# Value products of a whole pair of heads at a time, spatial mixing placed earlier, and first-norm vectors by float32r products

## The chip, the cores and the metric

The kernel runs on one core of one Trainium2 chip. The metric is device microseconds of one execution, launch to end; the profiled execution also has a span, the time from its first to its last instruction. TensorE (PE) does the matrix products and the transpositions, with its weight loads as a row of their own (PEld); VectorE (DVE), ScalarE (ACT) and GpSimd (POOL) do the element work; SyncE (SP) and ACT issue the transfers. Each engine runs its instructions in the order in which the program has them, and waits at an instruction whose inputs are not there.

## The reference, cut to what matters

```python
D_MODEL, SEQ, DEPTH = 1024, 512, 2          # x is (1, 512, 1024) float32

def gqa_attention(q, k, v):                 # 8 query heads of 64, 2 key/value heads, no mask
    sc = einsum('bqkgd,bskd->bkgqs', qi, k) * scale
    p = softmax(sc, axis=-1)
    return einsum('bkgqs,bskd->bqkgd', p, v)

def spatial_gating(u, v, ln_g, ln_b, w_s, b_s):   # 4 chunks of 128 rows, 8 groups of 64 columns
    vn = layer_norm(v, ln_g, ln_b)
    mixed = einsum('gmn,bcngd->bcmgd', w_s, vc) + b_s
    return u * mixed

def hybrid_layer(x, ...):
    hcat = x @ w_in + b_in
    na_q, na_k, na_v, na_z, gq_q, gq_k, gq_v, gq_z, sg_u, sg_v, sg_z, gates = split(hcat)
    p_a = (neighbourhood_attention(na_q, na_k, na_v) * silu(na_z)) @ w_br_a
    p_b = (gqa_attention(rope(rms_norm(gq_q)), rope(rms_norm(gq_k)), gq_v) * silu(gq_z)) @ w_br_b
    p_c = (spatial_gating(sg_u, sg_v) * silu(sg_z)) @ w_br_c
    g = sigmoid(gates)
    merged = g[0] * p_a + g[1] * p_b + g[2] * p_c
    return layer_norm(alpha * x + merged @ w_out + b_out, ln_g, ln_b)

h = layer_norm(x, ln_in_g, ln_in_b)         # the first norm
for l in range(DEPTH):
    h = hybrid_layer(h, ...)
```

## The kernel before, in words

All activations stay on the chip. A projection of float32 accuracy is three float32r products, high by high, low by high and high by low (L196, L197, L198), where the high part is a rounded copy made on ACT (`whi_*`, L143; `xh`, L249) and the low part the rest, made on DVE (`wlo_*`, L144; `xl`, L250). Weights come in chunks of 128 x 1024 (512 KB), eight (or four) of them to a projection, each in turn loaded by SP, split on ACT and DVE and multiplied.

**Order of the work.** `main` hands steps to a scheduler (`step(...)`), which fixes the order of the instructions of each engine when the program is built. The loop of one layer (from L928) first hands over ten chunks, the values of the spatial gating `sg_value`, those of the neighbourhood attention `na_value` and the first two gates of branch B (`zb_0`, `zb_1`), with the norms, rotations and stacking of the GQA queries and keys between them (list `between`, L934). Then come 16 units of GQA, one to a pair of heads `hp` (0 to 3) and a chunk of 128 queries `t` (0 to 3), with projections and the spatial mixing put between their steps (list `fill`, L944).

**One GQA unit** has, for the two heads e = 0, 1 of the pair: scores `gs` (L703 and L704, 512 keys), the row maximum `nm` on DVE (L706), Exp to `gp` with its row sum on ACT (L709), the division on DVE (`ri` L715, `gp` L716), four transpositions into one PSUM tile `gt` (L723) and its copy `gpT` to SBUF on ACT (L725, a ring of six buffers). After every second unit (`n % 2 == 0`, L962) the value products of the two units before it are handed over: `gqa_value`, tile `gy` (L735), which for each block of 128 keys has one product for e = 0 that writes the upper 64 partitions and one for e = 1 that writes the lower 64. A float32 product leaves two records in the trace, so one unit has 16 records of `gy`, which start two by two.

**Spatial gating**, `sg_mix(l, c)` for the four chunks c: `norm` transposes the projected values into PSUM (`svT`, L524) and takes their statistics on DVE (`st_sg`, L223 to L226); `mix` normalises by two DVE instructions (`vn`, L233 and L235), multiplies by the spatial weights (`mix`, L536, eight products of 64 columns, in the same two halves as `gy`) and adds the bias on DVE (L540, four instructions).

**Neighbourhood attention** comes later, between the projections of gates and branches: scores `ns`, transpositions `nT` with their copies to `npT` (two buffers of 128 x 896, L792 to L798), and value products `ny` (L810, L817), again in two halves.

**The start**, `first_layer_start` (L319): gain and bias of the first norm come as one row (`lnrow`, 8 KB, L323); four float32 products with a row of ones (`lnb`, L347) spread them over 128 partitions in PSUM; DVE applies them to the first rows of x (L359 and L361, twice each); then the transpositions `xt_in` (L365) and the first query products `gq` (L306). The raw weights are split by `high` (ACT, L337) and `low` (POOL for q0 and q1, DVE for q2 and q3, L340). The statistics of a norm end on POOL with a power (`rs_*`, L226).

## Time and profile before

| | |
|---|---|
| median of 3 runs | 1092.2 us (1090.23 to 1094.16) |
| the profiled execution, its own time | 1090.98 us |
| its span | 1089.2 us |
| busy share of PE, PEld, DVE, ACT, POOL | 99%, 82%, 59%, 43%, 5% |
| chain of work that ended last | PE 97%, DVE 2% |
| mean granted clock of TensorE | 0.998 of 2.4 GHz |

The span is the measure for the sum of a change, because starts and lengths are given in it. Matrix products overlap in the pipeline, so that the length of one in the trace (0.39 us for 512 columns) is longer than its distance to the next one's start (0.23 us); distances between starts are what a product costs. A busy PE in these rows is one with a product in the pipeline, which leaves room for bubbles between starts that no wait shows.

### The profile page before, as it was taken

The numbers are of one execution on the slowest core, as the hardware profiler recorded it, in microseconds if no ns is written. First come the engines' busy times: TensorE is split into PE (matmuls) and PEld (weight loads), VectorE is DVE, ScalarE is ACT, GpSimd is POOL, SyncE is SP. The second block draws the span as 40 slices with busy tenths as digits, with TensorE's granted clock in tenths as the row PEclk, the third lists the DMA queues.
The fourth block names the chain that finished last, engine by engine and source line by source line (L and its number), as shares of the span: only waits on it lengthen the run. The fifth ranks groups of instructions, "written<-read, shape, count | busy, mean of one in ns | idle before, by whom it ended". The sixth has DMA issues, their size and how long they took to land.

```text
span 1089.2 us, 14738 instructions
## 1 busy us (share of the span) xinstructions
PE 1075.7 (99%) x5744; PEld 887.8 (82%) x5744; DVE 640.5 (59%) x1205; ACT 470.6 (43%) x841; POOL 52.8 (5%) x54
## 2 busy tenths in 40 slices
PE   8999999999999999999999999999999999999997
PEld 5988788888888888888888887888888888888886
DVE  6775956665554543546876478566555555344465
ACT  4245735555655422334422365455645643223320
POOL 4420000000000000000021000000000000000001
PEclk9999999999999999999999999999999999999999
DMA  7522322213333433335652332222233334333421
GB/s 284 165 78 82 100 97 59 59 55 91 115 111 117 137 97 97 108 105 174 231 180 58 97 110 73 78 58 58 86 102 87 115 117 135 97 97 97 135 78 58
DMA packets 142808, 116.59 MB, mean 107 GB/s; under 512 B 4881, under 2 KB 130321, under 8 KB 142737
## 3 DMA queue, kind: packets, MB, share of 16 engines
q1 hardware_dynamic: 141872, 113.21, 33.5%
q10 hardware_dynamic: 866, 2.43, 0.6%
q8 instruction: 45, 0.74, 0.3%
q14 instruction: 25, 0.20, 0.1%
HBM read 109.34 MB, written 6.29 MB: 106 GB/s over the span
## 4 chain that ended last, share of the span: by engine, by line
PE 97%; DVE 2%; DMA 0%; issue 0%; ACT 0%; DVEq 0%
PE gq L306 4%; PE gy L735 3%; PE gb L196 3%; PE gc L198 3%; PE gc L197 3%; PE po L198 3%; PE po L197 3%; PE po L196 3%; PE gc L196 3%; PE ga L198 3%; PE ga L196 3%; PE gb L198 3%; PE gb L197 3%; PE ga L197 3%; PE gt L723 3%; PE gs L703 2%
## 5 line engine op out<-in xcount | busy, mean ns | idle before, releaser
L706 DVE TENSOR_REDUCE nm<-gs 128x1 f32<-128x512 f32 x64 | 42.3, 684 | 26.9 <-PE gs L704 26.8
L709 ACT ACTIVATE gp<-gs,nm 128x512 f32<-128x512 f32 x64 | 43.8, 688 | 21.4 <-DVE nm L706 19.8
L198 PE MATMUL gc<-xh,wlo_gc 128*128 128x512 f32 x128 | 51.1, 399 | 0.0
L725 ACT ACTIVATE gpT<-gt 128x512 f32<-128x512 f32 x64 | 36.7, 598 | 31.0 <-PE gt L723 30.8
L197 PE MATMUL gc<-xl,whi_gc 128*128 128x512 f32 x128 | 50.0, 391 | 0.0
L196 PE MATMUL gc<-xh,whi_gc 128*128 128x512 f32 x128 | 50.0, 391 | 0.0
L196 PE MATMUL gb<-xh,whi_gb 128*128 128x512 f32 x128 | 50.0, 391 | 0.0
L198 PE MATMUL gb<-xh,wlo_gb 128*128 128x512 f32 x128 | 49.8, 389 | 0.0
L197 PE MATMUL gb<-xl,whi_gb 128*128 128x512 f32 x128 | 49.8, 389 | 0.0
L196 PE MATMUL ga<-xh,whi_ga 128*128 128x512 f32 x128 | 49.8, 389 | 0.0
L198 PE MATMUL ga<-xh,wlo_ga 128*128 128x512 f32 x128 | 49.8, 389 | 0.0
L197 PE MATMUL ga<-xl,whi_ga 128*128 128x512 f32 x128 | 49.8, 389 | 0.0
L226 POOL TENSOR_TENSOR rs_po<-rs_po,pw 128x1 f32<-128x1 f32 x8 | 7.5, 939 | 814.4 <-DVE rs_po L225 814.4
L143 ACT ACTIVATE whi_gb<-raw_gb 128x1024 fp32r<-128x1024 f32 x16 | 17.0, 1060 | 60.4 <-PE pb L197 22.7
L779 ACT ACTIVATE nt<-nt,mx 128x256 f32<-128x256 f32 x64 | 30.1, 471 | 23.3 <-DVE mx L775 22.7
L144 DVE TENSOR_TENSOR wlo_ga<-raw_ga,whi_ga 128x1024 fp32r<-128x1024 f32 x16 | 19.6, 1222 | 33.5 <-ACT whi_ga L143 33.5
L735 PE MATMUL gy<-gpT,gv 128*64 128x128 f32 x512 | 38.8, 279 | 0.0
L723 PE MATMUL gt<-ident,gp 128*128 128x128 f32 x256 | 37.4, 276 | 0.7 <-ACT gpT L725 0.7
L735 PEld LDWEIGHTS gy<-gpT,gv 128*64 128x64 f32 x512 | 29.6, 136 | 10.2 <-issue 8.3
L144 DVE TENSOR_TENSOR wlo_gb<-raw_gb,whi_gb 128x1024 fp32r<-128x1024 f32 x16 | 19.6, 1222 | 30.1 <-ACT whi_gb L143 29.9
L723 PEld LDWEIGHTS gt<-ident,gp 128*128 128x128 f32 x256 | 29.7, 140 | 8.6 <-issue 2.7
L306 PE MATMUL gq<-w_gq,xh 128*128 128x512 f32 x128 | 34.0, 398 | 0.0
(282 smaller groups left out, 3099.0 us busy)
## 6 DMA issues: line engine op xcount, KB each, us to landing
raw_o<-in_w_out SPq DMA_DIRECT2D x24, 512.0 KB
raw_gc<-in_w_in SPq DMA_DIRECT2D x16, 512.0 KB
raw_gb<-in_w_in SPq DMA_DIRECT2D x16, 512.0 KB
raw_ga<-in_w_in SPq DMA_DIRECT2D x16, 512.0 KB
raw_gq<-in_w_in SPq DMA_DIRECT2D x8, 512.0 KB
raw_sv<-in_w_in SPq DMA_DIRECT2D x8, 512.0 KB
raw_nv<-in_w_in SPq DMA_DIRECT2D x8, 512.0 KB
raw_zb<-in_w_in SPq DMA_DIRECT2D x8, 512.0 KB
```

The costliest lines, as they stand in the source:

```text
L144: dve.tensor_tensor(wlo, raw, asf(whi), op=ALU.subtract)
L196: pe.matmul(ps, lhsT=lhi, rhs=rhi, start=first, stop=False)
L197: pe.matmul(ps, lhsT=lhi, rhs=rlo, start=False, stop=False)
L198: pe.matmul(ps, lhsT=llo, rhs=rhi, start=False, stop=last)
L306: pe.matmul(ps, lhsT=x[:, k, tk], rhs=w[p][k], start=n + k == 0, stop=n == 2 and k == KD - 1)
L703: pe.matmul(ps, lhsT=lhs, rhs=st["ks"][:, g, 0, :], start=True, stop=False)
L706: dve.tensor_reduce(out=nm, in_=ps, axis=AX.X, op=ALU.max, negate=True)
L709: act(pt, ps, AF.Exp, bias=nm, accum_out=sm)
L723: pe.transpose(ps[:, P * k:P * k + P], pt[:, P * k:P * k + P], ident)
L725: act(pT, ps, AF.Copy)
L735: pe.matmul(ps[64 * e:64 * e + 64, P * t:P * t + P], lhsT=st["gv"][:, k, HD * g:HD * g + HD], rhs=st["gp", hp, t, e][:, P * k:P * k + P], ...
L779: act(T[:, cs], T[:, cs], AF.Exp, bias=mx[:, i:i + 1], scale=SCALE, accum_out=sm[:, i:i + 1])
```

## The change

It has four parts. (1) The start: gain and bias are loaded spread over 128 partitions (`lnflat`, 256 KB instead of 8 KB), rounded on ACT, their rest taken on POOL, and `lnb` becomes eight float32r products over 32 partitions each, with ones of 1/32. (2) The low part of weight chunk q3 goes from DVE to POOL, ahead of the second statistics. (3) `gqa_value` is handed over once per pair of heads, four units together, the ring `gpT` has nine buffers, and `npT` takes two buffers of that ring instead of its own. (4) The norms and mixes of the spatial gating are handed over one by one between projections, the first before `zb_0` and before `zb_1`, and the third gate of B, `zb_2`, comes earlier.

```diff
@@ -86,8 +86,8 @@
     pw = cst.tile([P, 10], F32, name="pw")
     pool.memset(pw, -0.5)
 
-    one = cst.tile([P, 1], F32, name="one")
-    pool.memset(one, 1.0)
+
+
     bcol = cst.tile([P, DEPTH, NCOL], F32, name="bcol")
     hcol = cst.tile([P, DEPTH, NCOL], F32, name="hcol")
     bvg = cst.tile([P, DEPTH, NKV], F32, name="bvg")
@@ -319,8 +319,12 @@
     def first_layer_start():
         raw = {}
         input_load(0)
-        rows = rp.tile([P, 2, D], F32, tag="r8", name="lnrow")[0:1]
-        scalar.dma_start(rows, a["ln_in_rows"])
+        rows = rp.tile([P, 3, S], F32R, tag="r8", name="lnrow")
+        one = rows[:, 2, 0:P]
+        pool.memset(asf(one), 1.0 / 32)
+        R = a["ln_in_rows"]
+        flat = t2("lnflat")
+        scalar.dma_start(flat, bass.AP(tensor=R.tensor, offset=R.offset, ap=[[S, 4], [0, 32], [1, S]]))
         scalar.dma_start(ident, a["ident"])
         for n in ("q0", "q1", 1, "q2", "q3", 2, "k0", 3, "k1"):
             if isinstance(n, int):
@@ -341,11 +345,16 @@
 
         gains = {}
         lnc = st["lnc"] = cst.tile([P, 2, D], F32, tag="cvec", name="lnc_in")
-        for h in range(2):
-            for j in range(2):
-                ps = gains[j, h] = psum("acc" if h + j < 2 else "att", f"lnb_{h}_{j}")
-                pe.matmul(ps, lhsT=one[0:1].broadcast_to([1, P]), rhs=rows[:, j, 512 * h:512 * h + 512],
-                          start=True, stop=True)
+        act(rows[:, 0], flat, AF.Copy)
+        pool.tensor_tensor(rows[:, 1], flat, asf(rows[:, 0]), op=ALU.subtract)
+        for p in range(2):
+            for h in range(2):
+                for j in range(2):
+                    q = 64 * h + 32 * j
+                    if p == 0:
+                        gains[j, h] = psum("acc" if h + j < 2 else "att", f"lnb_{h}_{j}")
+                    pe.matmul(gains[j, h], lhsT=one[q:q + 32], rhs=rows[q:q + 32, p],
+                              start=p == 0, stop=p == 1)
 
         def stats(i):
             st["stats", i] = row_stats(st["xin", i], D, f"in{i}")
@@ -377,9 +386,9 @@
         apply(0)
         high("q2")
         low("q2", dve)
+        high("q3")
+        low("q3", pool)
         stats(1)
-        high("q3")
-        low("q3", dve)
         for kc in range(4):
             st["gqw", kc] = w[f"q{kc}"]
         gq_queries(0, 0)
@@ -721,7 +730,7 @@
         ps = psum("att", f"gt_{l}_{hp}_{t}_{e}")
         for k in range(NT):
             pe.transpose(ps[:, P * k:P * k + P], pt[:, P * k:P * k + P], ident)
-        pT = tp.tile([P, S], F32, tag="gpT", name=f"gpT_{l}_{hp}_{t}_{e}", bufs=6)
+        pT = tp.tile([P, S], F32, tag="gpT", name=f"gpT_{l}_{hp}_{t}_{e}", bufs=9)
         act(pT, ps, AF.Copy)
         st["gp", hp, t, e] = pT
 
@@ -789,13 +798,14 @@
 
     def na_transpose(l, hp, e):
         T = st["np", hp, e]
-        pT = tp.tile([P, 896], F32, tag="pT", name=f"npT_{l}_{hp}_{e}", bufs=2)
+        pT = []
         for j, n in ((0, 4), (1, 3)):
             ps = psum("att", f"nT_{l}_{hp}_{e}_{j}")
             for k in range(n):
                 c = P * (4 * j + k)
                 pe.transpose(ps[:, P * k:P * k + P], T[:, c:c + P], ident)
-            act(pT[:, 512 * j:512 * j + P * n], ps[:, 0:P * n], AF.Copy)
+            pT.append(tp.tile([P, S], F32, tag="gpT", name=f"npT_{l}_{hp}_{e}_{j}", bufs=9))
+            act(pT[j][:, 0:P * n], ps[:, 0:P * n], AF.Copy)
         st["np", hp, e] = pT
 
     def na_out(l, hp):
@@ -809,13 +819,13 @@
                     h = 2 * hp + e
                     pe.matmul(ps[64 * e:64 * e + 64, P * i + 64:P * i + 192],
                               lhsT=v[:, i + kb, HD * h:HD * h + HD],
-                              rhs=st["np", hp, e][:, 256 * i + P * kb:256 * i + P * kb + P],
+                              rhs=st["np", hp, e][i // 2][:, 256 * (i % 2) + P * kb:256 * (i % 2) + P * kb + P],
                               start=kb == 0, stop=kb == 1)
         for q0, kt, c in ((448, 3, 768), (0, 0, 832)):
             for e in range(2):
                 h = 2 * hp + e
                 pe.matmul(ps[64 * e:64 * e + 64, q0:q0 + 64], lhsT=v[:, kt, HD * h:HD * h + HD],
-                          rhs=st["np", hp, e][:, c:c + 64], start=True, stop=True)
+                          rhs=st["np", hp, e][1][:, c - 512:c - 448], start=True, stop=True)
         u = t2(f"nyo_{l}_{hp}")
         dve.scalar_tensor_tensor(out=u, in0=ps, scalar=bias(l, C_NAV + P * hp), in1=st["zs", "a", hp],
                                  op0=ALU.add, op1=ALU.mult)
@@ -930,19 +940,20 @@
         step(lambda l=l: layer_constants(l))
         chunks = [sg_value(l, f) for f in range(4)] + [na_value(l, f) for f in range(4)]
         chunks += [z_gate(l, "b", C_GZ, j) for j in range(2)]
-        M, R, T = gq_moments, gq_rotate, gq_stack
-        between = [[(M, 0)], [(M, 1)], [(R, 0)], [(T, 0), (M, 2)], [(R, 1)], [(T, 1), (M, 3)], [(R, 2)],
-                   [(T, 2), (R, 3)], [(T, 3)], []]
+        norm, mix = [list(fs) for fs in zip(*[sg_mix(l, c) for c in range(NCHUNK)])]
+        M, R, T = [[lambda i=i, f=f, l=l: behind_start(l, f, i) for i in range(NT)]
+                   for f in (gq_moments, gq_rotate, gq_stack)]
+        between = [[M[0]], [M[1]], [R[0]], [T[0], M[2]], [R[1]], [T[1], M[3]], [R[2]], [T[2], R[3]],
+                   [T[3], norm[0]], [mix[0], norm[1]]]
         for c, fs in zip(chunks, between):
-            for f, i in fs:
-                step(lambda l=l, f=f, i=i: behind_start(l, f, i))
+            for f in fs:
+                step(f)
             step(*c)
-        (n0, m0), (n1, m1), (n2, m2), (n3, m3) = [[(f,) for f in sg_mix(l, c)] for c in range(NCHUNK)]
         z = {j: z_gate(l, "b", C_GZ, j) for j in (2, 3)}
         u = [sg_out_u(l, j) for j in range(4)]
         g = [sg_out_z(l, j) for j in range(4)]
-        fill = [n0, na_q(l, 0), n1, m0, n2, na_k(l, 0), m1, n3, m2, m3, u[0], u[1], g[0], u[2], z[2], g[1],
-                u[3], z[3], g[2], g[3]]
+        fill = [na_q(l, 0), (mix[1],), (norm[2],), na_k(l, 0), (mix[2],), (norm[3],), z[2], (mix[3],), u[0], u[1], g[0],
+                u[2], g[1], u[3], z[3], g[2], g[3]]
         units = [(hp, t) for hp in range(NPAIR) for t in range(NT)]
         at = done = 0
         total = sum(len(f) - 1 for f in fill)
@@ -959,8 +970,8 @@
                 step(*fill[at])
                 done += len(fill[at]) - 1
                 at += 1
-            if n > 0 and n % 2 == 0:
-                for u in units[n - 2:n]:
+            if n > 0 and n % NT == 0:
+                for u in units[n - NT:n]:
                     step(lambda l=l, u=u: gqa_value(l, *u))
 
         rest = []
@@ -1046,7 +1057,7 @@
     arrays = {n: np.ascontiguousarray(v[n]) for n in _DIRECT}
     arrays["x"] = np.ascontiguousarray(v["x"].reshape(ROWS, 8, 8, D).transpose(1, 0, 2, 3).reshape(S, D))
     arrays["b_cols"] = np.ascontiguousarray(v["b_in"].reshape(DEPTH, NCOL, P).transpose(2, 0, 1))
-    arrays["ln_in_rows"] = np.ascontiguousarray(np.stack([v["ln_in_g"], v["ln_in_b"]])[None])
+    arrays["ln_in_rows"] = np.ascontiguousarray(np.stack([v["ln_in_g"], v["ln_in_b"]]).reshape(2, 2, S).transpose(1, 0, 2))
     bv = v["b_in"][:, C_GV:C_GV + P].reshape(DEPTH, NKV, HD).transpose(2, 0, 1)
     arrays["b_gv"] = np.ascontiguousarray(np.concatenate([bv, bv], axis=0))
     arrays["rpb"] = np.ascontiguousarray(np.pad(v["na_rpb"][:, :, ::-1, :], ((0, 0), (0, 0), (0, 0), (RPB_PAD, RPB_PAD))))
```

Lines move by up to 11: `gs` is L712 and L713 after the change, `nm` L715, `gt` L732, `gy` L744, `mix` L545, `svT` L533, `lnb` L356; L143 to L310 stay.

**PE, the place of the first mixing product of layer 0.** `mix_0` is the mixing of chunk 0 and reads `vn_0`; `zb_0` and `zb_1` are gates of branch B, `nq_0` a projection of the neighbourhood queries, `gs_e_t` scores. Before, from the first gate's last product on:

```order
...
L524 MATMUL svT_0_997<-ident,sv_520 128x128 x4
L703 MATMUL gs_0_0_974<-ks_502,qs_0_500 128x512
L198 MATMUL zb_1_944<-xh,wlo_zb_1_903 128x512
...
L704 MATMUL gs_1_0_982<-ks_502,qs_0_500 128x512
L196 MATMUL nq_0_1016<-xh,whi_nq_0_938 128x512
...
L198 MATMUL nq_0_1016<-xh,wlo_nq_0_939 128x512
L524 MATMUL svT_1_1049<-ident,sv_520 128x128 x4
L536 MATMUL mix_0_1064<-sgc_493,vn_0_1061 64x128 x8
```

Now:

```order
L498 MATMUL kT_636<-ident,qk_3_750 128x128
L533 MATMUL svT_0_909<-ident,sv_526 128x128 x4
L196 MATMUL zb_0_927<-xh,whi_zb_0_851 128x512
...
L713 MATMUL gs_0_1_1167<-ks_508,qs_0_506 128x512
L712 MATMUL gs_1_1_1175<-ks_508,qs_0_506 128x512
L713 MATMUL gs_1_1_1175<-ks_508,qs_0_506 128x512
L545 MATMUL mix_0_960<-sgc_499,vn_0_957 64x128 x8
L533 MATMUL svT_1_973<-ident,sv_526 128x128 x4
L196 MATMUL zb_1_991<-xh,whi_zb_1_921 128x512
```

`svT_0` moved ahead of the 24 products of `zb_0`, and `mix_0` ahead of the 24 of `zb_1` and the 24 of `nq_0`: between `kT` and `mix_0` there are now `svT_0`, `zb_0` and eight products of scores. Layer 1 has the same order.

**DVE, the instructions that end in `vn_0`.** `ks` and `qs` are the low parts of stacked keys and queries, `nm_e_t` row maxima of scores, `wlo_nq_0` the low part of a weight chunk. Before:

```order
L505 TENSOR_TENSOR ks_502<-kT_630,ks_502 64x512
L496 TENSOR_TENSOR qs_1_501<-qT_3_880,qs_1_501 64x2x128
L223 BN_STATS st_sg_0_1002<-svT_0_997 128x6
L144 TENSOR_TENSOR wlo_nq_0_939<-raw_nq_0_797,whi_nq_0_938 128x1024
...
L233 SCALAR_TENSOR_TENSOR vn_0_1061<-svT_0_997,mv_sg_0_1003,sgc_493 128x512
L706 TENSOR_REDUCE nm_0_0_977<-gs_0_0_974 128x1
L706 TENSOR_REDUCE nm_1_0_985<-gs_1_0_982 128x1
L235 SCALAR_TENSOR_TENSOR vn_0_1061<-vn_0_1061,rs_sg_0_1004,sgc_493 128x512
```

Now:

```order
L514 TENSOR_TENSOR ks_508<-kT_636,ks_508 64x512
L505 TENSOR_TENSOR qs_1_507<-qT_3_886,qs_1_507 64x2x128
L233 SCALAR_TENSOR_TENSOR vn_0_957<-svT_0_909,mv_sg_0_915,sgc_499 128x512
L715 TENSOR_REDUCE nm_0_0_1024<-gs_0_0_1021 128x1
L144 TENSOR_TENSOR wlo_nq_0_986<-raw_nq_0_803,whi_nq_0_985 128x1024
L715 TENSOR_REDUCE nm_1_0_1032<-gs_1_0_1029 128x1
L715 TENSOR_REDUCE nm_0_1_1170<-gs_0_1_1167 128x1
L715 TENSOR_REDUCE nm_1_1_1178<-gs_1_1_1175 128x1
L235 SCALAR_TENSOR_TENSOR vn_0_957<-vn_0_957,rs_sg_0_916,sgc_499 128x512
```

The statistics of `svT_0` moved ahead of the last `ks`, and two more row maxima stand ahead of the second instruction of `vn_0`, the last of them that of the scores right ahead of `mix_0` on PE.

**POOL at the start.** `rs_in` is the power that ends the statistics of a row block. Before:

```order
L226 TENSOR_TENSOR rs_in_136<-rs_in_136,pw 128x1
L340 TENSOR_TENSOR w_gq_0_142<-raw_gq_0_107,w_gq_0_142 128x1024
L340 TENSOR_TENSOR w_gq_1_145<-raw_gq_1_109,w_gq_1_145 128x1024
L226 TENSOR_TENSOR rs_in_171<-rs_in_171,pw 128x1
```

Now:

```order
L349 TENSOR_TENSOR lnrow<-lnflat,lnrow 128x512
L226 TENSOR_TENSOR rs_in_142<-rs_in_142,pw 128x1
L344 TENSOR_TENSOR w_gq_0_148<-raw_gq_0_107,w_gq_0_148 128x1024
L344 TENSOR_TENSOR w_gq_1_151<-raw_gq_1_109,w_gq_1_151 128x1024
L344 TENSOR_TENSOR w_gq_3_175<-raw_gq_3_115,w_gq_3_175 128x1024
L226 TENSOR_TENSOR rs_in_180<-rs_in_180,pw 128x1
```

The rest of gain and bias stands ahead of the first power, and the low part of q3 ahead of the second.

## Rows read from the trace of the kernel before

**Rows 1.** The page: busy time, share of the span and instructions of each engine.

```profile
PE 1075.7 (99%) x5744; PEld 887.8 (82%) x5744; DVE 640.5 (59%) x1205; ACT 470.6 (43%) x841; POOL 52.8 (5%) x54
```

**Rows 2.** The waits of PE: line, releaser, us in total, times, longest.

```profile
PE lnb L347 <- DMA lnrow<-in_ln_in_rows: 3.5, 1, 3.5
PE xt_in L365 <- DVE xin L361: 1.8, 2, 0.9
PE gt L723 <- ACT gpT L725: 0.7, 2, 0.4
PE nk L196 <- DVE vn L233: 0.2, 1, 0.2
```

**Rows 3.** Timeline of PE at a value group: start, us, what.

```profile
182.97 0.39 PE L198 MATMUL sz<-xh,wlo_sz 128*128 128x512 f32 x1
183.29 1.97 PE L735 MATMUL gy<-gpT,gv 128*64 128x128 f32 x32
...
185.53 0.40 PE L704 MATMUL gs<-ks,qs 128*128 128x512 f32 x1
185.76 0.39 PE L703 MATMUL gs<-ks,qs 128*128 128x512 f32 x1
```

**Rows 4.** The same group, asked for a stretch inside it (183.7 to 184.6).

```profile
183.45 1.37 PE L735 MATMUL gy<-gpT,gv 128*64 128x128 f32 x22
```

**Rows 5.** Timeline of PE at a value group that holds one pair of records.

```profile
134.56 0.40 PE L704 MATMUL gs<-ks,qs 128*128 128x512 f32 x1
134.89 0.43 PE L735 MATMUL gy<-gpT,gv 128*64 128x128 f32 x2
135.25 0.50 PE L703 MATMUL gs<-ks,qs 128*128 128x512 f32 x1
135.59 0.40 PE L704 MATMUL gs<-ks,qs 128*128 128x512 f32 x1
```

**Rows 6.** Timeline of PE: the last key transposition and the first mixing of layer 0.

```profile
97.41 0.27 PE L489 MATMUL kT<-ident,qk 128*128 128x128 f32 x1
...
116.47 1.09 PE L536 MATMUL mix<-sgc,vn 128*64 128x128 f32 x16
```

**Rows 7.** Timeline of DVE from behind the last stacked keys to vn, layer 0.

```profile
104.89 0.42 DVE L496 TENSOR_TENSOR qs<-qT,qs 64x256 fp32r<-64x256 f32 x1
...
105.96 1.21 DVE L144 TENSOR_TENSOR wlo_nq<-raw_nq,whi_nq 128x1024 fp32r<-128x1024 f32 x1
...
109.57 1.29 DVE L706 TENSOR_REDUCE nm<-gs 128x1 f32<-128x512 f32 x2 [0.31 <-PE gs L704]
110.77 0.74 DVE L235 SCALAR_TENSOR_TENSOR vn<-vn,rs_sg,sgc 128x512 f32<-128x512 f32 x1
```

**Rows 8.** Timeline of the start, PE, DVE and POOL.

```profile
3.53 7.16 PE L347 MATMUL lnb<-lnrow,one 1*128 1x512 f32 x8 [3.53 <-DMA lnrow<-in_ln_in_rows]
...
7.30 4.66 POOL L340 TENSOR_TENSOR w_gq<-raw_gq,w_gq 128x1024 fp32r<-128x1024 f32 x2 [0.18 <-ACT w_gq L337]
...
9.02 0.75 DVE L359 SCALAR_TENSOR_TENSOR xin<-xin,mv_in,lnb 128x512 f32<-128x512 f32 x1 [0.90 <-PE lnb L347]
...
10.72 0.75 DVE L361 SCALAR_TENSOR_TENSOR xin<-xin,rs_in,lnb 128x512 f32<-128x512 f32 x1 [0.96 <-PE lnb L347]
...
12.42 1.80 PE L306 MATMUL gq<-w_gq,xh 128*128 128x512 f32 x4
...
14.06 1.09 PE L306 MATMUL gq<-w_gq,xl 128*128 128x512 f32 x4
```

**Rows 9.** Stretches: us, busy PE, PEld, DVE, ACT, POOL, granted clock, DMA share, GB/s.

```profile
10.00:12.00 2.00, 2.00 (x7) 1.19 (x7) 0.75 (x1) 0.23 (x1) 1.96 (x1) 1.00 1.03 406
...
1082.00:1084.00 2.00, 0.01 (x1) 0.00 (x0) 1.85 (x6) 0.00 (x0) 0.43 (x1) 1.00 0.00 0
1084.00:1086.00 2.00, 0.00 (x0) 0.00 (x0) 2.00 (x4) 0.00 (x0) 0.49 (x1) 0.89 0.00 0
```

**Rows 10.** Timeline of DVE: the four additions behind a mixing.

```profile
119.15 0.87 DVE L540 TENSOR_TENSOR m<-mix,sgc 128x128 f32<-128x128 f32 x4
```

## The prediction

> **What bounds the kernel now.** I read the page first. PE is busy for 1075.7 us, 99% of the span [rows 1], so nothing is gained by making another engine faster; time can only come from PE's own stream. The waits of PE come to 6.2 us in the whole execution: 3.5 for the first transfer, 1.8 for the first norm, 0.9 for a copy `gpT` and a `vn` [rows 2]. The third view is the timeline of PE, read by distances between starts. A product of 512 columns starts 0.23 us behind the one before it (185.76 less 185.53 [rows 3]). Inside a group of value products two records, one of each half, make a pair. The group of 32 ends at 183.29 + 1.97 = 185.26 [rows 3], the 22 records from 183.45 on end at 184.82 [rows 4], so the last 8, four pairs, take 0.44: 0.11 us a pair. What costs more is going in and out. From the product ahead of the group of 16 pairs to the second product behind it pass 185.53 - 182.97 = 2.56 us [rows 3], where paces alone give 0.23 + 16 x 0.11 + 0.23 = 2.22: 0.34, and 0.36 with one more digit, is the price of **one excursion** into half-width products and back. A group of a single pair makes it plain: 135.59 - 134.56 = 1.03 against 0.23 + 0.11 + 0.23 = 0.57 [rows 5], 0.46 for an excursion that also splits a unit.
>
> **Parts 3 and 4, excursions.** Walking the whole trace in this way, a layer has 22 excursions for `gy` and `mix`, nine at 0.36 and thirteen that split a unit at 0.40 to 0.46, together 8.6 us; and five for `ny`, 1.1 us. In the changed order I count eight for `gy` and `mix`: three mixes alone, three whole pairs of heads, and the first pair of heads in two pieces (one with the last mix in it). Six at 0.36 and two at 0.42 are 3.0 us. `ny` has one more than before, 0.45. Saved: 8.6 - 3.0 - 0.45 = 5.2 us a layer, **-10.4 us**. The number of products is the same, and the ring of nine buffers only has to hold the eight copies of a pair of heads and one more; the four units' copies, 0.6 us each on an ACT that is 43% busy [rows 1], are spread over the products of a whole pair. Bounds: -9 (each excursion at 0.31) to -12 (0.42).
>
> **Old waits.** The two `gt` waits and the `nk` wait [rows 2] stand where the second and third mix of before crowd the units. With mixes spread they go: **-0.9 us**; bounds 0 and -1.6.
>
> **Part 4, a new wait.** This is the step on which the result turns. `mix_0` was started at 116.47 [rows 6], while the `vn` that it reads was done at 110.77 + 0.74 = 111.5 [rows 7]: 5 us of slack, made by the 24 products of `zb_1` and the 24 of `nq_0` that stood ahead. In the new order these come behind it. Behind the last key transposition, at 97.41 [rows 6], PE has four transpositions of `svT` (0.5 us), 24 products of `zb_0` and eight of scores: 32 x 0.23 = 7.3. With the way into the half-width products and out of the transpositions it is ready for `mix_0` at about 105.5. DVE is not. Its clock there is set by the stacked keys, whose last instruction ends as `qs` starts, 104.89 [rows 7]; the small statistics instructions moved ahead of it add 0.1. Then come, in the new order, `qs` 0.42, the first `vn` 0.74, one row maximum 0.65, `wlo_nq` 1.21, three row maxima at 0.65, the second `vn` 0.74: 5.7 us, to about 110.7 [rows 7]. All their inputs from PE and ACT are there before their turn, save the last maximum's, whose scores end just ahead of `mix_0`. PE waits 110.7 - 105.5 = **5.2 us**, in each layer, since the order is the same in both: **+10.4 us**. Queued behind `mix_0` on PE are `svT_1`, `zb_1`, `nq_0` and everything after them, so nothing else fills the hole. Later `mix` instructions have between 5 and 11 us of products between their `svT` and themselves, and DVE ahead of them is shorter, so they wait for nothing. Bounds for both layers: +3.0 (below, first rival) to +13.
>
> **A second, small wait.** `zb_2` now follows `mix_2` with some ten products and eight transpositions between, and takes over a PSUM buffer that DVE's additions (0.87 for four [rows 10]) must leave; with a `wlo` of 1.21 [rows 7] and another instruction between them they end 2 to 3 us behind `mix_2`, PE comes after some 2.5. I take 0.4 a layer, **+0.8 us**; bounds 0 and +3.
>
> **Parts 1 and 2, the start.** `lnb` runs from 3.53 to 10.69; two of the four instructions of DVE's first apply wait 0.90 and 0.96 for it, and the last ends at 11.47 [rows 8]. In the new form: the transfer is 31 times as large, 248 KB more, 0.6 us at the 406 GB/s of this stretch [rows 9]; a rounded copy on ACT, a subtraction on POOL (2.33 for 128 x 1024 in [rows 8], so about 1.2 for half of it), and eight products, together ready at about 7. Of the two waits, 1.86, I take 1.3 as gone, since the power that ends the statistics now stands behind the subtraction on POOL and holds the second instruction a little. Further on PE waits 1.8 us for the second apply [rows 2]. DVE reaches that apply 1.2 earlier, without q3's low part (1.21 for such an instruction [rows 7]); but the power on POOL that it needs now stands behind that same low part, 2.33 there, which cannot begin before ACT has rounded q3. So I let the second apply move by the same 1.3 and not more. The start gives **-1.3 us**; bounds +0.7 (the larger transfer late, POOL in the way) and -2.8.
>
> **The clock.** The last product of the program ends at 1082.01; the granted clock is 1.00 over 1082 to 1084 with PE idle, and 0.89 over 1084 to 1086 [rows 9], so it fell from 2.4 to 1.2 GHz towards the end of that second stretch. A wait of 5.2 us at `mix_0` would reach past that. What low clock costs is in the start: four products start over 14.06 - 12.42 = 1.64 us, 0.41 each, where the pace later is 0.23 [rows 8, 3], a loss of 0.72 for the four; the transpositions ahead of them are slow too. I take twice that for one fall, and one fall for the two waits: **+1.5 us**; bounds 0 and +7 (two falls, each for 14 products and more).
>
> **The sum.** -10.4 - 0.9 + 10.4 + 0.8 - 1.3 + 1.5 = +0.1 on the profiled execution's 1090.98: 1091.1, rounded to **1091.0 us**. That execution stands 1.2 us (0.1%) below the median of the three runs shown, inside their spread. About 0.3% (3.3 us) is what a measurement of this kernel can tell from no change.
>
> **Rivals.** (1) *The wait at `mix_0` is short.* The least that it can be: the last row maximum needs the last scores, so 0.65 + 0.74 [rows 7] and the hand-over follow PE's own work, 1.5 us a layer, if DVE is otherwise done. Then the clock stays too: 1091.1 - 2 x (5.2 - 1.5) - 1.5 = **1082 us**. For it: DVE is only 59% busy, and small shifts of ACT and DVE ahead of the keys would come through at once; against it: seven of the eight instructions behind the keys take 0.65 or more, and DVE runs them with no gap over 0.31 [rows 7]. (2) *The clock falls in both waits*, at `mix_0` of both layers, decided by whether the clock goes down within the wait as it did in the idle end of the run. It costs 3.0 us a layer if the low stretch is twice as long as I took it, 1091.1 - 1.5 + 6.0 = **1096 us**, slower than before. For it: the end of the run [rows 9] where the clock held for less than 5.2 us; against it: one fall at the end says little on how sharp the point is, and the half-width products and transpositions that follow the wait are cheap to slow. The Trainium skill, page "TensorE: Matmul & The Clock Gate", section "What's actually happening", has the array's clock gated to half once it has been idle and released by sustained work; by that rule both waits fall and this rival is the forecast. The end of this trace agrees with the fall, and no row here shows one in the middle of a run. (3) *Excursions are saved and the start fails*: +0.7 in place of -1.3, **1093 us**, no change.
>
> **How the numbers follow.** Forecast with rival 3, a balance of the saved excursions and the new wait: 0.50. Rival 1 or something between it and the forecast, below 1087.7 (1091.0 less 3.3): 0.27. Rival 2, above 1094.3: 0.23. The range reaches from rival 1 to rival 2 with its bounds on the excursions, 1082 to 1097.5. Faster 0.27, within 0.3% 0.50, slower 0.23.
>
> **What would show it.** The waits of PE should have a new row, `mix` for DVE's `vn` at L235, two times, near 5 us each, and those of `gt` and `nk` should be gone; `xt_in` should wait about as long as before, with the first `gq` 1.3 us earlier; a granted clock below 1.00 in a stretch just behind one of the waits; groups of 32 `gy` records, 28 excursions in place of 54. The forecast is wrong if the `mix` wait is under 3 us, if excursions inside long groups cost more than 0.36, or if another wait above 2 us stands behind a `gt`, `nT` or `zb`.

## The result, and the profile after

| | before | after |
|---|---|---|
| median of the timed runs | 1091.45 us (5 runs) | 1100.68 us (5 runs, 1099.9 to 1100.99) |
| the profiled execution, its own time | 1090.98 us | 1099.9 us |
| its span | 1089.2 us | 1097.7 us |
| PE waits, sum of the rows | 6.2 us | 25.5 us |

The changed kernel is slower: the ratio is 1.0082 (95% interval 1.0068 to 1.0095), 9 us. The forecast was 1091.0 us and a range to 1097.5; the time is above both.

The waits of PE after the change, to be read against [rows 2]: line, releaser, us in total, times, longest.

```profile
PE lnb L356 <- ACT lnrow L348: 11.5, 1, 11.5
PE mix L545 <- DVE vn L235: 9.2, 2, 4.6
PE xt_in L374 <- DVE xin L370: 3.3, 4, 1.7
PE gt L732 <- ACT gpT L734: 1.0, 2, 0.6
PE lnb L356 <- POOL lnrow L349: 0.5, 1, 0.5
```

Two rows are new and large. The wait of `mix` for `vn` is the one that was forecast, twice 4.6 us. The first row was not: `lnb` waits 8 us longer than before for its vectors. PE is busy for 10.9 us less than before [rows 1], 5.6 of them in `lnb` itself (7.16 before, two times 0.80 now), and for all that the span is longer:

```profile
PE 1064.8 (97%) x5744; PEld 889.1 (81%) x5744; DVE 642.1 (58%) x1204; ACT 470.1 (43%) x842; POOL 56.1 (5%) x56
```

What was saved, and more, went into waiting. The timeline of the start after the change (start, us, engine, what; the bracket is the idle time before and what ended it), which answers to [rows 8]:

```profile
10.67 0.34 SPq L131 DMA_DIRECT2D xin<-in_x  x1
10.68 0.63 ACT L348 ACTIVATE lnrow<-lnflat 128x512 fp32r<-128x512 f32 x1 [7.04 <-DMA lnflat<-in_ln_in_rows]
...
11.39 1.28 POOL L349 TENSOR_TENSOR lnrow<-lnflat,lnrow 128x512 fp32r<-128x512 f32 x1 [9.27 <-ACT lnrow L348]
...
12.72 0.80 PE L356 MATMUL lnb<-lnrow 32*128 32x512 f32 x4 [0.47 <-POOL lnrow L349]
...
17.52 2.06 PE L306 MATMUL gq<-w_gq,xh 128*128 128x512 f32 x4
```

The vectors land at 10.67, not near 4. ACT stands still for 7 us, SP's next load goes out only at the same moment, and the first full product starts at 17.52 in place of 12.42. Meanwhile the weights come in slowly. One stretch, 4 to 10 us, of before and then of after (us, busy PE, PEld, DVE, ACT, POOL, granted clock, DMA share, GB/s):

```profile
4.00:10.00 6.00, 6.00 (x8) 1.99 (x6) 3.80 (x7) 2.11 (x2) 3.25 (x3) 1.00 1.05 396
```

```profile
4.00:10.00 6.00, 0.00 (x0) 0.00 (x0) 1.65 (x4) 0.00 (x0) 0.00 (x0) 1.00 1.07 265
```

The mixing of chunk 0 in layer 0, PE after the change, against [rows 6]:

```profile
110.02 0.47 PE L712 MATMUL gs<-ks,qs 128*128 128x512 f32 x1
110.32 0.40 PE L713 MATMUL gs<-ks,qs 128*128 128x512 f32 x1
115.34 1.97 PE L545 MATMUL mix<-sgc,vn 128*64 128x128 f32 x16 [4.62 <-DVE vn L235]
117.24 1.12 PE L533 MATMUL svT<-ident,sv 128*128 128x128 f32 x4
118.01 0.78 PE L196 MATMUL zb<-xh,whi_zb 128*128 128x512 f32 x1
118.58 0.63 PE L197 MATMUL zb<-xl,whi_zb 128*128 128x512 f32 x1
119.01 0.52 PE L198 MATMUL zb<-xh,wlo_zb 128*128 128x512 f32 x1
119.37 0.40 PE L196 MATMUL zb<-xh,whi_zb 128*128 128x512 f32 x1
```

and DVE ahead of it, against [rows 7]:

```profile
109.90 0.42 DVE L505 TENSOR_TENSOR qs<-qT,qs 64x256 fp32r<-64x256 f32 x1
110.35 0.75 DVE L233 SCALAR_TENSOR_TENSOR vn<-svT,mv_sg,sgc 128x512 f32<-128x512 f32 x1
111.02 0.68 DVE L715 TENSOR_REDUCE nm<-gs 128x1 f32<-128x512 f32 x1
111.62 1.21 DVE L144 TENSOR_TENSOR wlo_nq<-raw_nq,whi_nq 128x1024 fp32r<-128x1024 f32 x1
112.75 1.88 DVE L715 TENSOR_REDUCE nm<-gs 128x1 f32<-128x512 f32 x3
114.55 0.74 DVE L235 SCALAR_TENSOR_TENSOR vn<-vn,rs_sg,sgc 128x512 f32<-128x512 f32 x1
```

These are the eight instructions of the forecast, back to back, 109.90 to 115.29: 5.4 us. The granted clock over these microseconds (same columns as above):

```profile
112.00:113.00 1.00, 0.00 (x0) 0.00 (x0) 1.00 (x2) 0.52 (x2) 0.00 (x0) 0.72 0.00 0
113.00:114.00 1.00, 0.00 (x0) 0.00 (x0) 1.00 (x3) 0.53 (x1) 0.00 (x0) 0.50 0.03 9
...
118.00:119.00 1.00, 1.00 (x4) 0.82 (x3) 0.99 (x5) 0.00 (x0) 0.00 (x0) 0.50 0.36 104
119.00:120.00 1.00, 1.00 (x5) 0.86 (x4) 0.96 (x3) 0.00 (x0) 0.00 (x0) 0.87 0.47 134
```

The clock goes down during the wait and is still down for four microseconds of work: the mixing, four transpositions and three products run at about half pace. In layer 1 the chain and the wait (4.62) have the same lengths, and two products more are slow behind it:

```profile
650.44 1.98 PE L545 MATMUL mix<-sgc,vn 128*64 128x128 f32 x16 [4.62 <-DVE vn L235]
...
655.29 0.40 PE L198 MATMUL zb<-xh,wlo_zb 128*128 128x512 f32 x1
```

Last, a value group after the change, against [rows 3]:

```profile
190.60 0.39 PE L198 MATMUL sz<-xh,wlo_sz 128*128 128x512 f32 x1
190.92 3.71 PE L744 MATMUL gy<-gpT,gv 128*64 128x128 f32 x64
194.56 0.50 PE L712 MATMUL gs<-ks,qs 128*128 128x512 f32 x1
194.90 0.40 PE L713 MATMUL gs<-ks,qs 128*128 128x512 f32 x1
```

64 records, a whole pair of heads, in one group: 194.90 - 190.60 = 4.30 us, against 0.23 + 32 x 0.11 + 0.23 = 3.98 by paces, so 0.32. A group of twice the length pays about the same price for going in and out, once.

### The profile page after: what moved, and what is told of

It is laid out like the page before. It is cut to its first block, busy times and chain, and to the rows that moved or that the text cites. A ratio compares the mean times of both kernels' runs of the same rounds, so it can differ in the third digit from the quotient of the medians.

```text
span 1097.7 us, 14742 instructions
## 1 busy us (share of the span) xinstructions
PE 1064.8 (97%) x5744; PEld 889.1 (81%) x5744; DVE 642.1 (58%) x1204; ACT 470.1 (43%) x842; POOL 56.1 (5%) x56
## 4 chain that ended last, share of the span: by engine, by line
PE 93%; DVE 2%; DMA 2%; ACT 1%; issue 1%; POOL 0%; SPq 0%; DVEq 0%; POOLq 0%; ACTq 0%
PE gq L306 3%; PE gy L744 3%; PE gc L196 3%; PE po L197 3%; PE gb L196 3%; PE gc L197 3%; PE po L198 3%; PE po L196 3%; PE gc L198 3%; PE ga L196 3%; PE gb L198 3%; PE ga L198 3%; PE gb L197 3%; PE ga L197 3%; PE gt L732 2%; PE su L196 1%
## 5 line engine op out<-in xcount | busy, mean ns | idle before, releaser
L715 DVE TENSOR_REDUCE nm<-gs 128x1 f32<-128x512 f32 x64 | 41.7, 681 | 10.9 <-PE gs L713 10.8
L143 ACT ACTIVATE whi_gb<-raw_gb 128x1024 fp32r<-128x1024 f32 x16 | 17.0, 1060 | 60.4 <-PE pb L197 22.7
L144 DVE TENSOR_TENSOR wlo_ga<-raw_ga,whi_ga 128x1024 fp32r<-128x1024 f32 x16 | 19.5, 1222 | 33.5 <-ACT whi_ga L143 33.5
L732 PE MATMUL gt<-ident,gp 128*128 128x128 f32 x256 | 36.3, 273 | 1.0 <-ACT gpT L734 1.0
L732 PEld LDWEIGHTS gt<-ident,gp 128*128 128x128 f32 x256 | 30.6, 140 | 7.3 <-ACT gpT L734 1.5
L143 ACT ACTIVATE whi_ga<-raw_ga 128x1024 fp32r<-128x1024 f32 x16 | 17.0, 1061 | 37.9 <-PE ga L197 22.6
L725 DVE TENSOR_SCALAR gp<-gp,ri 128x512 f32<-128x512 f32 x64 | 30.2, 482 | 1.5
```

The source lines that it names most:

```text
L143: act(whi, raw, AF.Copy)
L144: dve.tensor_tensor(wlo, raw, asf(whi), op=ALU.subtract)
L715: dve.tensor_reduce(out=nm, in_=ps, axis=AX.X, op=ALU.max, negate=True)
L725: dve.tensor_scalar(out=pt, in0=pt, scalar1=ri, scalar2=None, op0=ALU.mult)
L732: pe.transpose(ps[:, P * k:P * k + P], pt[:, P * k:P * k + P], ident)
```

## The experiments

Times are medians; a ratio is against runs of the kernel before on the same chip. "Start", "value" and "mix" stand for parts 1 and 2, part 3 and part 4 of the change.

| kernel | what it is | median us | ratio, 95% interval | PE waits for `mix` |
|---|---|---|---|---|
| e1_start_old | value + mix | 1094.0 | 1.0019 (1.0009 to 1.0029) | 9.2 |
| e2_start_new | start | 1098.0 | 1.0065 (1.0048 to 1.0082) | 0 |
| e4_value_only | value | 1092.9 | 1.0016 (1.0002 to 1.0031) | 2.0, and 5.5 at `gt` |
| e4b_mix_only | mix | 1103.1 | 1.0107 (1.0092 to 1.0122) | 9.3 |
| e3_mix_late | value + mix, first mix later | 1081.8 | 0.9912 (0.9897 to 0.9927) | 1.9 |
| e7_vn_early | value + mix, `vn` earlier on DVE | 1079.4 | 0.9891 (0.9876 to 0.9905) | 0 |
| e9_nq_pool | value + mix, one DVE instruction less | 1090.6 | 0.9993 (0.9984 to 1.0003) | 7.0 |
| e6_rows_apart | start, other place and pattern | 1092.1 | 1.0013 (1.0000 to 1.0025) | 0 |
| e12_copies_first | start, other pattern | 1091.6 | 0.9999 (0.9989 to 1.0008) | 0 |
| e13_apart_four | start, other place | 1097.9 | 1.0054 (1.0039 to 1.0069) | 0 |
| e5_start_small | start, 4 packets, 4 transfers | 1095.2 | 1.0037 (1.0024 to 1.0050) | 0 |
| e10_four_rows | start, 4 packets, 1 transfer | 1092.4 | 1.0013 (1.0004 to 1.0023) | 0 |
| e11_best | e7_vn_early with the start of e10 | 1080.0 | 0.9894 (0.9878 to 0.9911) | 0 |

### The parts apart

**e1_start_old.** The changed kernel with the functions of the start as they were.

> The changed kernel with the start of before (parts 1 and 2 undone), value products and mixes as changed. Theory A, the parts add: the start of the changed kernel costs 4.9 us (first full product at 17.5 in place of 12.4 us, steady at 26.8 in place of 21.9), so 1100.7 - 4.9 = about 1095.8 us, with the mix wait still 4.6 us twice and the clock still low behind it. Theory B, the late start is taken back later because DVE and the transfers have more time: about 1100 us, mix wait longer than 4.6 us.

1094.0 us, 6.7 below the changed kernel, and the mix wait is 9.2 us as in the changed kernel: theory A, with more gained than the 4.9 expected. The new start costs at least what it delays. (In the profiled execution of this kernel the first transfer landed 0.9 us earlier than in that of before, so that `sv`, the second projection, begins 5.9 us earlier than in the changed kernel, 50.64 against 56.51. The spans differ by 5.4 only: behind the two waits the clock stays low over two to three products more than in the changed kernel.)

**e2_start_new.** The kernel before with the new start.

> The kernel before with parts 1 and 2 alone (the new start). Theory A, the whole loss of the start is in the landing of the spread vectors, 10.7 us in place of 3.5: first full product 5 us later, time 5 to 7 us above before, about 1097 us. Theory B, it needed the other parts: within 1 us of before.

1098.0 us: theory A. `lnb` waits 12.3 us for the rounded vectors. The start's loss needs none of the other parts. In the profiled execution `sv` begins 5.8 us later than before, and the span is 7.0 longer: 0.6 of the difference is that `gt` waits 1.3 us in place of 0.7, the rest no row shows.

**e4b_mix_only.** The kernel before with the lists of part 4.

> The kernel before with part 4 alone (norms and mixes handed over between projections). Theory A: 52 excursions in place of 54, so -0.8 us, and the whole of the new wait, 2 x 4.6, with 2 x 2.0 for the low clock behind it: about 1091.4 + 12.4 = 1104 us. Theory B, the wait comes only with the other parts (late weights of the start, or the longer groups): within 2 us of before.

1103.1 us: theory A, within 1 us of the number. Alone, the new order of the mixes is the worst of the three parts.

```profile
PE mix L536 <- DVE vn L235: 9.3, 2, 4.6
```

**e4_value_only.** The kernel before with part 3.

```diff
-            if n > 0 and n % 2 == 0:
-                for u in units[n - 2:n]:
+            if n > 0 and n % NT == 0:
+                for u in units[n - NT:n]:
```

> The kernel before with part 3 alone (value products once per pair of heads, ring of nine, npT in the ring). Theory A: 54 excursions become 30, 24 fewer at 0.36 to 0.42 us, and no mix wait: about 1091.4 - 9.5 = 1082 us, granted clock 1.00 throughout. Theory B, long groups hold back copies or transpositions: new waits of gt or nT of several us, 1088 us or more.

1092.9 us: theory A fails by 11 us. The time is theory B's, the cause is not: no copy or transposition was held back by a long group. There are 24 excursions fewer, but waits for DVE stand in their place:

```profile
PE gt L723 <- DVE rs_sg L225: 2.9, 2, 1.5
PE gt L723 <- DVE gp L716: 2.6, 2, 1.3
PE mix L536 <- DVE m L540: 2.0, 2, 1.0
```

They come once in each layer, where the second and third mix of before stand among the first units. There, by the order of before, the value products of two units were work that PE did while DVE made `vn`, maxima and additions. With the value products moved behind the fourth unit, PE arrives early at each of these. Behind three waits of 1.0 to 1.5 us, between 132.0 and 137.5, the clock goes down as well (row of 138 to 140 us of this kernel):

```profile
138.00:140.00 2.00, 2.00 (x21) 1.98 (x22) 1.62 (x5) 0.60 (x1) 0.13 (x1) 0.56 0.00 0
```

So the parts do not add. Part 4 removes these waits and puts one longer wait at the first mix; without part 4, part 3 is worth nothing.

### The wait at the first mix

**e3_mix_late.** As e1, with the first mix behind `zb_1`.

```diff
-                   [T[3], norm[0]], [mix[0], norm[1]]]
+                   [T[3], norm[0]], []]
...
-        fill = [na_q(l, 0), (mix[1],), (norm[2],), na_k(l, 0), (mix[2],), (norm[3],), z[2], (mix[3],), u[0], u[1], g[0],
+        fill = [(mix[0],), (norm[1],), na_q(l, 0), (mix[1],), (norm[2],), na_k(l, 0), (mix[2],), (norm[3],), z[2], (mix[3],), u[0], u[1], g[0],
```

> The changed kernel with the start of before, and the first mix and second norm handed over one chunk later, behind zb_1 in place of ahead of it. Theory A, the wait is only a matter of the place: PE has 5.5 us more to do, the wait falls below 0.7 us a layer, the clock stays at 1.00, time about 1081 us (30 excursions). Theory B, DVE's chain to vn is pushed later with it: a mix wait of several us stays, 1088 us or more.

1081.8 us: theory A. The clock stays at 1.00, and a wait of 1.0 us a layer remains, where the expectation had 0.7. Its row names ACT:

```profile
PE mix L536 <- ACT zsb L583: 1.9, 2, 1.0
```

but ACT's `zsb` is not an input of `mix`; in the same timeline DVE's second `vn` ends at 111.66 and `mix` starts at 111.76, so it is `vn` here too, two of whose row maxima ahead now wait for scores.

**e7_vn_early.** As e1, with the two instructions of `vn` handed over in `norm`, so that DVE makes them right behind the statistics. On PE the mixes stay ahead of `zb_1` as in the change; the last two products of scores, which stood ahead of `mix_0`, come behind it in this program.

```diff
             st["vp", c] = ps, row_stats(ps, SGW, f"sg{l}_{c}")
+            vn = st["vn", c] = t2(f"vn_{l}_{c}")
+            norm_apply(vn, ps, SGW, st["sg"][2], st["sg"][3], st["vp", c][1])
...
-            vn = t2(f"vn_{l}_{c}")
-            norm_apply(vn, ps, SGW, slg, slb, stats)
+            vn = st["vn", c]
```

> The changed kernel with the start of before and with the two instructions that make vn handed over with the statistics (in norm) in place of with the mix; the mixes stay ahead of zb_1. On DVE vn of chunk 0 then ends ahead of the last stacked keys and of all row maxima. Theory A, the mix wait comes from DVE's order, not from svT or from the amount of work: wait of mix for vn gone, clock 1.00, scores wait up to 1 us a layer for the later keys, about 1082 us. Theory B, DVE has too much to do there in any order: waits of 3 us a layer or more turn up at the scores, 1088 us or more.

1079.4 us: theory A, and 2.6 better than expected; up to 2 of that is the wait of the scores, which does not appear. The second `vn` of chunk 0 is done at 104.42, and `mix_0` starts at 104.92 without a wait:

```profile
103.67 0.75 DVE L235 SCALAR_TENSOR_TENSOR vn<-vn,rs_sg,sgc 128x512 f32<-128x512 f32 x1
```

All that PE waits for in this kernel stands at the start:

```profile
PE lnb L347 <- DMA lnrow<-in_ln_in_rows: 3.6, 1, 3.6
PE xt_in L365 <- DVE xin L361: 1.6, 2, 1.0
```

The same transpositions, the mix still ahead of `zb_1` on PE and even two products earlier, the same work on DVE: the wait was DVE's order. This is the best version of all that were run, 1.1% faster than before.

**e9_nq_pool.** As e1, with one 1.2 us instruction of that DVE chain, the low part of the first chunk of `nq`, on POOL.

```diff
-            dve.tensor_tensor(wlo, raw, asf(whi), op=ALU.subtract)
+            (pool if name in ("nq0_0", "nq1_0") else dve).tensor_tensor(wlo, raw, asf(whi), op=ALU.subtract)
```

> As e1_start_old, but the low part of the one weight chunk that stands among DVE's row maxima ahead of vn (1.1 us there) is made on POOL; the order of everything else stays. The mix wait should fall from 4.6 to about 3.5 us in each layer. Theory A, the clock still falls in a wait of 3.5 us: 1094.0 - 2 x 1.1 = about 1091.8 us, mean clock 0.992. Theory B, the clock stays up: 2 x 1.8 us more are saved, about 1088 us, mean clock 0.998. Theory C, the wait has another cause: no change from 1094 us.

The wait falls to 3.5 us as expected: what is taken off DVE's chain comes off PE's wait, and theory C is out. The time, 1090.6 us, lies between A (1091.8) and B (1088), nearer to A. The clock does fall, only later and for a shorter time:

```profile
109.00:110.00 1.00, 1.00 (x15) 0.83 (x12) 0.97 (x6) 0.00 (x0) 0.00 (x0) 0.91 0.66 197
110.00:111.00 1.00, 1.00 (x4) 0.81 (x4) 1.00 (x4) 0.00 (x0) 0.00 (x0) 0.50 0.28 69
...
113.00:114.00 1.00, 1.00 (x5) 0.84 (x4) 0.87 (x3) 0.00 (x0) 0.55 (x1) 0.89 0.19 55
```

In this kernel `mix` starts at 108.38 and runs at full pace (16 records in 1.0 us); the clock goes down at about 109.8, when PE has been back at work for more than a microsecond.

### The start

**e6_rows_apart.** As e2, with every one of the 128 rows at a place of its own in memory.

```diff
-        scalar.dma_start(flat, bass.AP(tensor=R.tensor, offset=R.offset, ap=[[S, 4], [0, 32], [1, S]]))
+        scalar.dma_start(flat, bass.AP(tensor=R.tensor, offset=R.offset, ap=[[32 * S, 4], [S, 32], [1, S]]))
```

> As e2_start_new, but each of the 128 rows of the spread vectors is read from a place of its own in memory (the input holds every row 32 times), same 128 packets of 2 KB, same queue. Theory A, 128 packets that read the same 8 KB are slow and slow the weights with them (250 GB/s in place of 390 over 4 to 10 us): the vectors land at 4.5 to 5.5 us and the time is 1 us below to 1 us above before. Theory B, the packets are late because they take turns with the weights on the transfer engines: landing near 10.7 us and time as e2_start_new, about 1097 us.

1092.1 us and a landing at 5.47: it looked like theory A. But the pattern here, 4 x 32 rows without gaps, is one run of 128 rows, so that two things had changed: the place that is read and the outermost count of the pattern.

```profile
5.47 0.63 ACT L348 ACTIVATE lnrow<-lnflat 128x512 fp32r<-128x512 f32 x1 [2.55 <-DMA lnflat<-in_ln_in_rows]
```

**e12_copies_first** and **e13_apart_four** separate them: the first reads the same 8 KB with the copies outermost, the second reads rows apart with a gap that keeps an outermost count of four.

```diff
-ap=[[S, 4], [0, 32], [1, S]]
+ap=[[0, 32], [S, 4], [1, S]]
```

```diff
-ap=[[S, 4], [0, 32], [1, S]]
+ap=[[33 * S, 4], [S, 32], [1, S]]
```

> As e2_start_new, the same 8 KB read by 128 packets, but the access pattern of the load has the 32 copies as its outermost step and the four rows inside it, so that the outermost count is 32 and not 4. (The rows land interleaved, so the first norm's gain and bias are not the reference's in this kernel; every transfer and instruction after it is the same.) Theory A, many packets that read one place in memory are slow: landing near 10 us, 250 GB/s, about 1097.5 us as e2_start_new. Theory B, an outermost count of 4 put all 128 packets on four transfer engines: landing at about 5.5 us as in e6_rows_apart, about 1092 us.

> As e6_rows_apart, every one of the 128 packets reads a place of its own, but the copies of the four rows are 33 rows apart in memory, so that the pattern keeps an outermost count of 4 (in e6_rows_apart the pattern was one run of 128 rows). Theory A (one place in memory): landing at about 5.5 us, about 1092 us as e6_rows_apart. Theory B (four transfer engines): landing near 10 us, about 1097.5 us as e2_start_new.

Both go theory B's way. e12 lands at 5.07 and takes 1091.6 us, e13 lands at 11.14 and takes 1097.9 us. The row of ACT in the timeline of e12, with its first full product, then the row of ACT in e13:

```profile
5.07 0.63 ACT L348 ACTIVATE lnrow<-lnflat 128x512 fp32r<-128x512 f32 x1 [1.76 <-DMA lnflat<-in_ln_in_rows]
...
11.90 2.06 PE L306 MATMUL gq<-w_gq,xh 128*128 128x512 f32 x4
```

```profile
11.14 0.63 ACT L348 ACTIVATE lnrow<-lnflat 128x512 fp32r<-128x512 f32 x1 [7.52 <-DMA lnflat<-in_ln_in_rows]
```

and the stretch of 4 to 10 us of e12, then of e13 (the last number is GB/s):

```profile
4.00:10.00 6.00, 1.97 (x10) 0.99 (x11) 3.57 (x7) 2.74 (x3) 4.13 (x4) 1.00 1.04 396
```

```profile
4.00:10.00 6.00, 0.00 (x0) 0.00 (x0) 1.65 (x4) 0.00 (x0) 0.00 (x0) 1.00 1.07 257
```

Reading one place 32 times costs nothing that shows; an outermost count of four costs 6 us and a third of the rate of all transfers together. The Trainium skill, page "DMA: Bandwidth & Descriptors", section "Rules for kernel authors", says that the outermost step of a transfer's pattern sets over how many of the 16 transfer engines it is spread, and that an outermost count below 16, such as that of a leading broadcast, confines it to at most that many. These two runs agree with it by their landings, 5.07 and 11.14; which engines moved a packet stands in no row here.

**e5_start_small.** As e2, with four packets of 2 KB in four transfers over zeros, ones of 1.0.

> As e2_start_new, but only four packets of 2 KB are loaded, one to a group of 32 partitions over zeros, with ones of 1.0 in place of 1/32; rounding, subtraction and the eight float32r products stay. Theory A, the products and the two element steps are quick and only the large transfer cost time: the vectors land near 3.5 us, the first full product comes 1 us or more before the 12.4 us of before, time 1 to 2 us below before. Theory B, the row-group products or the subtraction on POOL are the cost: no gain, 1091 us or more.

1095.2 us, but the run says little on either theory: four issues and the transfer of `ident` behind them held ACT's queue from 1.4 to 5.3 us, and the vectors were complete at 8.97 only. What was small was not early.

**e10_four_rows.** The same in one transfer.

```diff
+        dve.memset(flat, 0.0)
-        scalar.dma_start(flat, bass.AP(tensor=R.tensor, offset=R.offset, ap=[[S, 4], [0, 32], [1, S]]))
+        scalar.dma_start(flat[0:P:32], bass.AP(tensor=R.tensor, offset=R.offset, ap=[[S, 4], [1, S]]))
```

> As e5_start_small, but the four packets of 2 KB go in one transfer in place of four, so that the issue does not hold ACT's queue. Theory A, with the vectors landed near 3.5 us the new products are worth what was forecast: first full product near 11.1 us in place of 12.4, time 1 to 1.5 us below before. Theory B, the second apply on DVE and POOL's power take it back: first product earlier, but the steady stretch from 21.9 us on starts at most 0.5 us earlier and the time is within 0.7 us of before.

1092.4 us. The landing near 3.5 that both theories began from did not come about, it was 5.66; the first full product starts at 12.48, no earlier than before, so theory A was not put to its own condition. Together with e6 and e12 it shows what the start is worth with vectors at 5.1 to 5.7 us: the first full product starts at 11.9 to 12.5, and the time is 0.1% above or equal to that of before in all three. In their profiled executions `sv` begins 0.1 to 0.7 us earlier than before and the span is still 1.1 to 1.6 longer; `gt` waits 1.5 to 1.7 us in them in place of 0.7, and most of the rest no row shows.

**e11_best.** e7 with this start.

> e7_vn_early with the start of e10_four_rows in place of that of before. Theory A of e10: 1079.4 - 1.3 = about 1078 us. Theory B of e10: within 0.7 us of e7_vn_early, 1079 to 1080 us. Either way no mix wait and a clock at 1.00.

1080.0 us: theory B. This start, whose vectors land some two microseconds behind those of before, is worth nothing here either.

## Why the prediction was wrong

By its own terms, in us; "measured" is from the two profiled executions, whose spans differ by 8.5; for the start it is how much later the first product of `sv` begins (56.51 and 51.61).

| term | forecast | measured |
|---|---|---|
| excursions | -10.4 | -10.6 |
| old waits of `gt` and `nk` | -0.9 | +0.1 |
| new wait at `mix_0`, both layers | +10.4 | +9.2 |
| wait of `zb_2` | +0.8 | 0 |
| low clock | +1.5 | +4.0 |
| start | -1.3 | +4.9 |
| sum | +0.1 | +7.6 |

**The step that failed is the start.** The price of the new load was: "the transfer is 31 times as large, 248 KB more, 0.6 us at the 406 GB/s of this stretch". It took 7 us (10.67 against 3.53): the price was worked out by bytes, at the rate that all transfers together reach, and the access pattern of the load, which stood in the diff, was not looked at. (The load is 32 times as large, not 31; the 248 KB and the 0.6 us follow all the same.) The bound +0.7, with "the larger transfer late" in it, was too narrow by 4 us. With that one term at the measured 4.9 the forecast would have been 1097 us, with the 6.7 of e1 1099.

The step behind the landing was about right. From the landing to the first full product pass 17.52 - 10.68 = 6.8 us after the change, and as much in e12 (11.90 - 5.07), against 12.42 - 3.53 = 8.9 before [rows 8]: 2.1 us shorter. But even with the pattern repaired the vectors land at 5.07 to 5.66, 1.5 to 2.1 later than the one row of before, and not 0.6 later; so the first full product comes at most 0.5 us earlier (e6, e10, e12), and the time is not below that of before. No run landed the vectors near 4 us, so whether the -1.3 would have come then is not shown.

**The wait at `mix_0` was right**, in its place, its cause and its chain of eight instructions; 4.6 us in place of 5.2, because the chain took 5.4 us in place of 5.7 and the last scores waited 0.3 us for the stacked keys, so that PE came later. e7 and e9 show that the order on DVE alone makes it.

**The clock was mis-sized**, and rival 2 is what happened: the clock fell in both waits, not in one. The price in the forecast came from four slow products of the start, in stretches whose rows show a granted clock of 1.00 (12 to 14 us), so that no row showed them to be at low clock. The price is best read against e3, where mix, transpositions and products follow each other in the same order at full clock. From the start of the mix to that of the fourth product behind it pass 119.37 - 115.34 = 4.03 us after the change, and in e3

```profile
111.76 1.09 PE L536 MATMUL mix<-sgc,vn 128*64 128x128 f32 x16 [0.95 <-ACT zsb L583]
112.78 0.66 PE L524 MATMUL svT<-ident,sv 128*128 128x128 f32 x4
113.20 0.48 PE L196 MATMUL nq<-xh,whi_nq 128*128 128x512 f32 x1
...
113.98 0.40 PE L196 MATMUL nq<-xh,whi_nq 128*128 128x512 f32 x1
...
114.44 0.39 PE L198 MATMUL nq<-xh,wlo_nq 128*128 128x512 f32 x1
```

113.98 - 111.76 = 2.22: 1.8 us in layer 0. In layer 1, to the sixth product behind the mix, it is 655.29 - 650.44 = 4.85 against 114.44 - 111.76 = 2.68: 2.2 us. Together 4.0: two falls at about 2.0, where the forecast had one at 1.5 and rival 2 had two at 3.0. By the rule of the Trainium skill that the prediction named (page "TensorE: Matmul & The Clock Gate", section "What's actually happening"), that the clock is gated to half once the array has been idle, both waits would lower the clock. In this trace both did.

**The excursions were right to 0.2 us**: 54 excursions that cost 19.5 us became 28 that cost 8.9 once the wait and the low clock inside two of them, 5.6 each, are taken out of 20.1. What the prediction did not see is that this gain is not part 3's own: in e4, part 3 by itself, 7.5 us of waits stand where the value products were, and the time is no better than before.

**The old waits** went and came again in another form: `gt` waits 1.0 us in all. Of the 0.9 us by which the measured terms miss the difference of the spans, 0.6 is the wait of the last scores ahead of `mix_0` in the two layers; the rest was not broken down.

The errors of the other terms cancel for the most part, which is luck: clock +2.5, old waits +1.0, `mix_0` -1.2, `zb_2` -0.8, excursions -0.2, together +1.3.

Of the signs that the prediction named, the two `mix` waits, the low clock behind them and the 28 excursions came; the groups have 64 records and not 32, four units of 16. The first `gq`, which was to be 1.3 us earlier, is 5.1 later, and `xt_in` waits 3.3 us in place of 1.8. These two point at the start; none of the conditions under which the prediction called itself wrong did.

## What to carry to other kernels

A load is priced by its access pattern before its bytes: where the outermost count is small, put the many copies or partitions outermost, and see in the first microseconds whether everything else slowed with it. Work that is moved because it is expensive where it stands may be cover for another engine there; ask, for each place it leaves, which engine was catching up (e4), and for each place something new is wanted, where the maker of its input stands in its own queue (e7). When a consumer is moved forward, move its producer forward in the producing engine's order too: here that took 14.6 us off (1094.0 in e1, 1079.4 in e7).

## What the runs showed of the hardware that was not expected

A transfer of 256 KB with an outermost count of four landed at 10.7 to 11.5 us, with one of 32 or 128 at 5.1 to 5.5, at the same number and size of packets, and while it lasted all transfers together moved 257 to 269 GB/s in place of 395. The clock of TensorE went down in waits of 4.6 us, behind a wait of 3.5 us, and behind three waits of 1.0 to 1.5 us with a little work between; a single wait of 1.0 us (e3) left it at 1.00; behind the wait of 3.5 us it went down only when PE was at work again. In e7, where there is no such wait, the clock stays at 1.00 over the same work. So a profile can show low clock in a busy stretch when the wait that goes with it stands ahead.
